# Opening the attention's tile pools beside the last unit of the even layer's projections

## The chip, the cores and the metric

The kernel runs on one core of a Trainium2 chip. It is written with a tile framework: the program says which tiles exist and which instructions read and write them, and a planner puts every engine's instructions into one queue per engine. The core has a matrix engine (TensorE, PE, with a separate row PEld for its weight loads), three engines for elementwise work (VectorE = DVE, ScalarE = ACT, GpSimd = POOL) and SyncE (SP), which here only issues DMA transfers. The matrix engine writes into PSUM, which has eight banks; everything else lies in SBUF, which is shared out in pools of tiles.

The metric is the device time of one execution in microseconds, the median of several. Two profiles are compared by their span.

## The reference

The step runs a hybrid decoder of two layers over a prompt of 2048 tokens and over 8 sampled sequences of 4 tokens each. Layer 0 (the even layer) projects the normalised input once and gives half of the columns to a gated linear recurrence (HGRN2, four heads) and half to forgetting attention (FoX, four heads of 128). Layer 1 (the odd layer) is a second gated recurrence (GLA). What matters here is the attention:

```python
# prompt: causal softmax with a decay bias from the cumulated log forget gates c
logits = q @ k.T * scale + c[t] - c[s]          # masked to s <= t
out = softmax(logits) @ v                       # 16 blocks of 128 queries per head
# sample: the same over 2048 cached positions, gathered by page (16 pages of 128 for each
# of 8 sequences), and over the 4 new ones
out_s = softmax([q @ k_pages.T * scale + suffix, new]) @ [v_pages, v_new]
```

The projection of the even layer has 4 x 512 columns for HGRN2, 4 x 512 for FoX and 4 for the forget gates; afterwards the branches' outputs are joined and multiplied with the layer's output weights.

## The kernel before, in words

**The even layer.** `phase_even` (L1118) works on the prompt in two halves of 1024 tokens (the 32 sample tokens go with the first). For each half the 1024x4100 input weights are taken in 16 *units* of 256 columns, in the order of the list `order` (v0, g0, qf0, ..., Bk0, Bv0, Bk1, Bv1). A unit's product runs as three fp16 matmuls for each 128x128 block (high by high, high by low, low by high, lines L625 to L627 in `mm3`). The 32 units of both halves are numbered 0 to 31. The last, unit 31, is Bv1 of the second half: the value columns of heads 2 and 3. It has four steps of two token tiles; each leaves one PSUM bank of tag `pj` (three banks), which DVE and ACT empty (L1063, L1069, L1070, L1079), and SP stores the fp16 pairs to the scratch tensor `vd` (L1084).

**Key pages beside the units.** The sample's attention reads 128 cached key pages of 256 KB. They are worked on during the units, four pages at a time, 32 times. `KEYS` lists the step numbers (four per unit, 4 * unit + step) at which a load of four pages is issued. `ahead` (L1551) then does the rest at fixed distances: two and three steps later DVE turns the pages (L1526), four steps later the scores are multiplied (L1571), and after each second load the scores are stored five steps later (L1564). Page and turned page lie in the four buffers of tag `wr`, which also hold raw weights during the first half.

**The attention.** `phase_fox` (L1347) opens four pools after the even layer's pools are closed: `fe` and `fx` for tiles in SBUF, `fpa` and `fpb` for PSUM (tags s 2, sc 1; t 2, o 1, kt 2: eight banks). `fox_prompt` (L1365) is a generator for the prompt: for each of four heads, four groups G = 0..3 of 512 queries. A group loads its q, k, bias, v and gate (`loads`, five DMA issues on SP, L1377 to L1392), then for each of four query blocks makes G + 1 score banks (tag `s`), adds the bias and takes the maximum on DVE (L1412), exponentiates on ACT (L1420) and normalises on POOL (L1428). The values of a group (`values`, L1431) are traced among the scores of the next: PE turns the probabilities (L1448), ACT and DVE split them (L1455, L1456), PE multiplies them with v into tag `o`. `fox_sample` (L1598) is the generator for the sample: after a few loads and the masks built on POOL (`past`), it adds the forget bias to the key scores, takes the softmax, and multiplies 2 x 16 sets of four value pages (L1750, called the page steps below) and then the four new positions. Its last step copies and turns the result (L1759, L1762), stores it, and derives a scale for the next projection (L1768 to L1772).

**What sets the order.** Each generator yields a weight after every piece of work. `until(a, ta, b, tb)` draws from a and b so that their sums of weights stay in the proportion ta : tb, and ends when b ends; if a ends first, the rest of b follows. `mux` does the same until both are used up. In `phase_fox` prompt and sample are drawn 270000 : 500000. When the sample is through, `phase_odd` draws what is left of the prompt together with `prepare` (REST_P : REST_S), which loads and splits the first output weight unit (`w_o`: L337, then L355 to L363) and loads and splits the first two pieces of the layer's output `yT` into `act` (L1840, L1847 to L1854). The order of tracing is only a priority: the planner puts an instruction into its engine's queue when its model of time has it ready, the earlier traced first. `issue_after` holds an instruction behind a given one on the same engine. A page step may run ahead of its place, but not before the last matmul that was traced two page steps earlier (VAHEAD = 3).

**Memory.** Pools on the left side of SBUF and on the right side are stacks. Before, the even layer has act, w (three split weight buffers, the four `wr` buffers and small tags) and wl on the right; wk, nrm and stt on the left; and one PSUM pool with pj 3, gr 2, st 1, o 2. A tile in a newly opened pool waits only for the tiles whose bytes it covers.

Of the kernel before, what the change touches and what calls it, by code (L numbers as in the profile page):

```python
# [8 lines left out]
F32 = mybir.dt.float32  # L9
# [6 lines left out]
ALU = mybir.AluOpType  # L16
PSUM = bass.MemoryType.PSUM
DRAM = bass.MemoryType.DRAM

P = 128  # L20
# [18 lines left out]
EWR = 4  # L39
# [9 lines left out]
PG = 6  # L49
KEYS = (*range(4 * 13, 4 * 17, 4), *range(4 * 17, 4 * 31, 2))  # L50
LATER = (*range(4, 14), *range(17, 27))
# [3 lines left out]
FOX_S = 500000.0  # L55
FOX_P = 270000.0
LIN3_A = 40000.0
LIN_E = (20000.0, 15000.0)
# [6 lines left out]
FAR = -3e38  # L65
# [44 lines left out]
def drain(g):  # L110
    for _ in g:
        pass
# [11 lines left out]
class Kern:  # L124
# [993 lines left out]
    def phase_even(self):  # L1118
        tc, nc, i = self.tc, self.nc, self.i
        def pool(name, **kw):  # L1120
            return tc.tile_pool(name=name, bufs=1, reuse_waits="tile", **kw)

        with pool("act", side="right") as ap, pool("w", side="right") as w0, pool("wl", side="right") as wp1, \
                pool("wk") as wp0, pool("nrm") as n0, pool("stt") as sp, pool("ps", space=PSUM) as pp0:
            wpool = self.wpool = Pool(w0, {"w": 3, "wr": EWR, "rm": 3, "pow": 3, "lr": 1})
            wp = Pool(wp0, {"c4": 7, "sam": 1, "v4": 3, "sg": 3, "pd": 1, "kt": 2, "y": EY, "xpad": 1, "vs": 3,
                            "ss": 2, "rs_t": 2, "rs_r": 2, "qz": 1, "scs": 2}, Pool(wp1, {"c2": EC2, "th": ETH}))
            pps = Pool(pp0, {"pj": 3, "gr": 2, "st": 1, "o": 2})
            nrm = Pool(n0, {"th": 1, "nss": 4, "rs_t": 4, "rs_r": 4})
# [7 lines left out]
            last = iter(())  # L1137
# [16 lines left out]
            for hf in range(2):  # L1154
# [89 lines left out]
                last = dense(15, 16)  # L1244
            drain(last)
            for t in range(4 * 32, 4 * 32 + 2):
                self.ahead(wpool, pps, t)

# [78 lines left out]
    def log_sigmoid(self, pool, z, tag):  # L1327
# [17 lines left out]
        nc.vector.scalar_tensor_tensor(zz, q, -2.0, zz, ALU.mult, ALU.add)  # L1345

    def phase_fox(self):  # L1347
        tc, nc = self.tc, self.nc
        self.fox = ExitStack()
        f1, f0 = (self.fox.enter_context(tc.tile_pool(name=x, bufs=2, reuse_waits="tile")) for x in ("fe", "fx"))  # L1350
        pp1, pp0 = (self.fox.enter_context(tc.tile_pool(name=x, bufs=2, space=PSUM, reuse_waits="tile"))
                    for x in ("fpa", "fpb"))
        if True:
            fx = Pool(f0, {"P": 20},
                      Pool(f1, {"caus": 1, "q2": 3, "k2": 6, "cb": 2, "st1": 12, "cm": 2, "th": 4, "tl": 4, "y": 1, "v2": 6, "sg": 3}))
            pps = Pool(pp0, {"t": 2, "o": 1, "kt": 2}, Pool(pp1, {"s": 2, "sc": 1}))
            caus = fx.tile([P, P], F32, tag="caus", name="caus")
            nc.gpsimd.memset(caus, 0.0)
            nc.gpsimd.affine_select(caus, caus, [[-1, P]], ALU.is_ge, FAR, base=0, channel_multiplier=1)
            with tc.tile_pool(name="fs", bufs=1, side="right", reuse_waits="tile") as s0:  # L1360
                fs = Pool(s0, {"pg": PG, "kt": 2})
                self.prompt = self.fox_prompt(fx, pps, caus)
                drain(until(self.prompt, FOX_P, self.fox_sample(fs, pps), FOX_S))

# [233 lines left out]
    def fox_sample(self, fs, pps):  # L1598
# [4 lines left out]
        def one(shape, name, dt=F32):  # L1603
            return fs.tile(shape, dt, tag=name, name=name)
# [41 lines left out]
        def past():  # L1646

            with self.tc.issue_after(self.last_cm.ins):
# [18 lines left out]
                for h in range(NH):  # L1667
# [7 lines left out]
                                        base=0, channel_multiplier=1)  # L1675

            tots = one([P, NH], "tots")
            nc.vector.reduce_sum(tots, lfp.rearrange("p s h -> p h s"), axis=mybir.AxisListType.X)
# [583 lines left out]
```

## Time and profile before

| | |
|---|---|
| median of 3 runs | 2291.44 us (2286.28 to 2295.47) |
| the profiled execution | 2291.65 us |
| its span | 2289.9 us |
| TensorE clock granted, mean | 0.99 |
| PE busy | 2195.9 us (96%) |
| DVE, ACT, POOL busy | 1400.7, 994.3, 724.9 us |
| unit 31's products | 887.8 to 911.4 us |
| attention's first score | 914.5 us |
| first product with the output weights | 1239.0 us |

The span is the time from the first to the last instruction in the trace; the profiled execution lies 0.2 us above the median. A view by windows gives, for each stretch, the time each engine was busy in it with the number of instructions in brackets, then the clock that TensorE was granted (1.00 is full speed), the mean share of the DMA engines that was busy, and GB/s. In a list of instructions the square bracket says how long the engine was idle ahead of the instruction and what released it.

### The profile page before, as it was taken

What the parts mean: (1) busy time and instruction counts of PE and PEld (TensorE: products, weight loads), DVE (VectorE), ACT (ScalarE), POOL (GpSimd) and SP (SyncE); (2) the same over time, 40 slices, a digit from 0 to 9 for tenths busy, and PEclk for the clock granted to TensorE, in tenths of its full rate; (3) what the DMA queues carried; (4) which work ended last, traced back from release to release, by engine and by line L of the source; (5) the groups of instructions that cost most, each with busy time, mean ns of one, the idle gap of its engine ahead of it and who ended that gap; (6) DMA issues with size and microseconds to landing.
All of it is one profiled execution on the core that took longest, in us unless ns stands there. A gap on an engine that the chain in (4) does not pass through costs nothing.

```text
span 2289.9 us, 58071 instructions
## 1 busy us (share of the span) xinstructions
PE 2195.9 (96%) x23316; PEld 1569.0 (69%) x23316; DVE 1400.7 (61%) x3154; ACT 994.3 (43%) x2216; POOL 724.9 (32%) x787
## 2 busy tenths in 40 slices
PE   7999999999999999899999999999999999999998
PEld 5667667774575588455457888677677667567887
DVE  7767677735564466877776454366665655557454
ACT  5434434321221221566667353554644644555243
POOL 2233234100110111544445354154442422232232
PEclk9999999999999999999999999999999999999999
DMA  7444545796575475977735779324325421115554
GB/s 235 144 124 150 160 150 185 233 238 151 159 184 138 118 204 149 280 223 246 223 111 170 260 219 253 101 71 144 92 97 101 120 79 59 54 52 179 171 179 152
DMA packets 361984, 364.02 MB, mean 159 GB/s; under 512 B 108161, under 2 KB 305090, under 8 KB 357490
## 3 DMA queue, kind: packets, MB, share of 16 engines
q1 hardware_dynamic: 359570, 353.69, 52.7%
q0 software_dynamic: 2144, 6.62, 0.8%
q8 instruction: 183, 3.00, 0.6%
q14 instruction: 87, 0.71, 0.1%
HBM read 245.85 MB, written 97.47 MB: 150 GB/s over the span
## 4 chain that ended last, share of the span: by engine, by line
PE 42%; DVE 3%; ACT 2%; DMA 2%; POOL 2%; issue 1%; SPq 0%; POOLq 0%; DVEq 0%; ACTq 0%
PE pt_o L625 4%; PE pt_o L626 4%; PE pt_o L627 4%; PE pt_Cv L625 2%; PE pt_Cv L627 2%; PE pt_Cv L626 2%; PE o_C L909 1%; PE gl_C L756 1%; PE pt L1448 1%; POOL s_C L842 1%; PE py_C L728 1%; ACT L L1420 1%; DMA wr_o<-in_w_out_odd 1%; PE fo L626 0%; PE fo L627 0%
## 5 line engine op out<-in xcount | busy, mean ns | idle before, releaser
L625 PE MATMUL pt_o<-w_o,act 128*128 128x256 f16 x1024 | 279.4, 273 | 1.4 <-ACT sg1C L682 1.4
L626 PE MATMUL pt_o<-w_o,act 128*128 128x256 f16 x1024 | 279.7, 273 | 0.0
L627 PE MATMUL pt_o<-w_o,act 128*128 128x256 f16 x1024 | 279.3, 273 | 0.0
L625 PEld LDWEIGHTS <-act 128*128 128x128 f16 x2304 | 226.1, 98 | 42.3 <-issue 5.3
L626 PEld LDWEIGHTS <-act 128*128 128x128 f16 x2304 | 226.3, 98 | 31.3 <-issue 2.2
L627 PEld LDWEIGHTS <-act 128*128 128x128 f16 x2304 | 226.1, 98 | 31.4 <-issue 2.6
L789 POOL TENSOR_TENSOR kA<-kA,fA 128x512 f32<-128x512 f32 (+1 forms) x56 | 74.2, 1325 | 367.9 <-PE gl_A L756 307.5
L625 PE MATMUL pt_Cv<-w_Cv,act 128*128 128x256 f16 (+1 forms) x512 | 141.5, 276 | 0.9 <-DVE rh L1959 0.8
L627 PE MATMUL pt_Cv<-w_Cv,act 128*128 128x256 f16 (+1 forms) x512 | 141.4, 276 | 0.0
L626 PE MATMUL pt_Cv<-w_Cv,act 128*128 128x256 f16 (+1 forms) x512 | 141.3, 276 | 0.0
L1420 ACT ACTIVATE L<-L,nm,kc 128x512 f32<-128x512 f32 (+3 forms) x160 | 118.2, 741 | 39.4 <-DVE nm L1418 36.1
L1428 POOL TENSOR_SCALAR L<-L,nm 128x512 f32<-128x512 f32 (+3 forms) x160 | 98.2, 629 | 87.4 <-DVE nm L1424 33.7
L789 POOL TENSOR_TENSOR kC<-kC,fC 128x512 f32<-128x512 f32 (+1 forms) x56 | 81.8, 1461 | 136.6 <-PE gl_C L756 93.1
L1455 ACT ACTIVATE th<-pt 128x512 f16<-128x512 f32 (+3 forms) x159 | 80.9, 526 | 74.1 <-PE pt L1448 73.4
L1526 DVE STREAM_TRANSPOSE kt<-kp 128x512 f32<-128x512 f32 x128 | 82.1, 684 | 40.7 <-DMA kp<-in_cache_fox_k 39.7
L1456 DVE TENSOR_TENSOR tl<-pt,th 128x512 f16<-128x512 f32 (+3 forms) x159 | 94.4, 607 | 16.0 <-ACT th L1455 15.0
L1448 PE MATMUL pt<-ident,L 128*128 128x128 f32 x544 | 89.8, 280 | 9.0 <-DVE tl L1456 5.6
L1448 PEld LDWEIGHTS pt<-ident,L 128*128 128x128 f32 x544 | 65.8, 143 | 39.1 <-DVE tl L1456 10.1
L788 DVE TENSOR_TENSOR qC<-qC,fC 128x512 f32<-128x512 f32 (+1 forms) x56 | 72.9, 1302 | 21.1 <-PE gl_C L756 21.1
L1950 ACT ACTIVATE vC<-pt_Cv,kc 128x512 f32<-128x512 f32 (+1 forms) x40 | 23.9, 598 | 134.0 <-PE pt_Cv L627 134.0
L625 PE MATMUL pt_Bv<-w_Bv,act 128*128 128x260 f16 (+1 forms) x256 | 70.8, 277 | 3.9 <-DVE Bvs L1070 3.9
L363 POOL TENSOR_TENSOR w_o<-wr_o,w_o 128x512 f16<-128x512 f32 x32 | 46.5, 1467 | 79.1 <-ACT w_o L362 55.2
(959 smaller groups left out, 6460.4 us busy)
## 6 DMA issues: line engine op xcount, KB each, us to landing
kp<-in_cache_fox_k SPq DMA_DIRECT2D x128, 256.0 KB, 4.9
pgcache_fox_v<-in_cache_fox_v SPq DMA_DIRECT2D x128, 256.0 KB, 4.1
yr<-yT SPq DMA_DIRECT2D x16, 1024.0 KB, 7.0
x1d<-xo SPq DMA_DIRECT2D x44, 256.0 KB, 4.1
wr_o<-in_w_out_even SPq DMA_DIRECT2D x32, 256.0 KB, 5.5
xo<-in_x_prompt SPq DMA_DIRECT2D x32, 256.0 KB, 4.5
wr_Cv<-in_w_in_odd SPq DMA_DIRECT2D x32, 256.0 KB, 3.4
x1r<-x1d SPq DMA_DIRECT2D x16, 512.0 KB, 4.5
```

Source lines behind the costliest of these rows:

```text
L363: nc.gpsimd.tensor_tensor(lo, r, hi, ALU.subtract)
L625: nc.tensor.matmul(ps, lh[0], rh[0], start=first, stop=False)
L626: nc.tensor.matmul(ps, lh[0], rh[1], start=False, stop=False)
L627: return nc.tensor.matmul(ps, lh[1], rh[0], start=False, stop=last)
L788: nc.vector.tensor_tensor(xv[:, :, 1], xv[:, :, 1], t0.to_broadcast([P, nb, w]), ALU.mult)
L789: nc.gpsimd.tensor_tensor(kv[:, :, 0], kv[:, :, 0], t1.to_broadcast([P, nb, w]), ALU.mult)
L1420: self.last_exp = nc.scalar.activation(lt[:, :w], lt[:, :w], AF.Exp, bias=nm[:, 0:1], scale=ib, accum_out=nm[:, 2 + j : 3 + j])
L1428: nc.gpsimd.tensor_scalar(lt[:, :w], lt[:, :w], nm[:, 1:2], 2.0**14, ALU.mult, ALU.mult)
L1448: nc.tensor.transpose(pt[:, w : w + P], rows[b][s // 4][0][:, (s % 4) * P : (s % 4 + 1) * P], self.ident)
L1455: nc.scalar.activation(th[:, a:w], pt[:, a:w], AF.Copy),
L1456: nc.vector.tensor_tensor(tl[:, a:w], pt[:, a:w], th[:, a:w], ALU.subtract)))
L1526: return self.nc.vector.transpose(kt[:, :, 32 * x : 32 * x + 32], t[:, x].rearrange("p (a e) -> p a e", e=32))
```

## The change

The pools of the attention are opened ahead of the last unit instead of after it, and the prompt's generator is drawn beside that unit:

- In `phase_even` the pools are regrouped. The buffers `wr`, `rm`, `pow` and `lr` move from the right side to a new pool on the left; the PSUM tag `pj` (three banks) becomes a pool of its own. The left pools and the other five PSUM banks form an inner group, which is closed once unit 30 and the bias rows (L1312) are traced.
- `fox_open` then opens `fe` and `fx` on the left and one PSUM pool of five banks (t 2, o 1, s 2), and makes the causal mask and the prompt's generator. The tags kt 2 and sc 1, which only the sample and the prompt's end use, get their three banks in `phase_fox`, when `pj` is closed.
- Unit 31 is drawn as `until(self.prompt, FOX_A = 14000, last, 21120)`: the unit's four steps weigh 5280 each, so the prompt is given some 14000 of its weight until the unit has ended. Then `phase_fox` draws prompt and sample 270000 : 500000 as before, both sums starting at zero.
- `KEYS` is moved so that the last key pages are finished with unit 30: the steps were 52, 56, 60, 64, 68, then every second one from 70 to 122; they are 52, 56, 60, then every second one from 62 to 118.
- In `fox_sample`, a yield of 9000 stands between the masks on POOL and the matmuls that use them.

```diff
-KEYS = (*range(4 * 13, 4 * 17, 4), *range(4 * 17, 4 * 31, 2))
+KEYS = (4 * 13, 4 * 14, *range(4 * 15, 4 * 30, 2))
+FOX_A = 14000.0
...
         with pool("act", side="right") as ap, pool("w", side="right") as w0, pool("wl", side="right") as wp1, \
-                pool("wk") as wp0, pool("nrm") as n0, pool("stt") as sp, pool("ps", space=PSUM) as pp0:
-            wpool = self.wpool = Pool(w0, {"w": 3, "wr": EWR, "rm": 3, "pow": 3, "lr": 1})
+                pool("pj", space=PSUM, side="right") as pp1:
+            inner = ExitStack()
+            wk, wp0, n0, sp = (inner.enter_context(pool(x)) for x in ("wr", "wk", "nrm", "stt"))
+            pp0 = inner.enter_context(pool("ps", space=PSUM))
+            wpool = self.wpool = Pool(w0, {"w": 3}, Pool(wk, {"wr": EWR, "rm": 3, "pow": 3, "lr": 1}))
...
-            pps = Pool(pp0, {"pj": 3, "gr": 2, "st": 1, "o": 2})
+            pps = Pool(pp0, {"gr": 2, "st": 1, "o": 2}, Pool(pp1, {"pj": 3}))
...
-            drain(last)
-            for t in range(4 * 32, 4 * 32 + 2):
-                self.ahead(wpool, pps, t)
+            inner.close()
+            self.fox_open()
+            drain(until(self.prompt, FOX_A, last, 21120.0))
...
+    def fox_pool(self, name, **kw):
+        return self.fox.enter_context(self.tc.tile_pool(name=name, bufs=2, reuse_waits="tile", **kw))
+
+    def fox_open(self):
+        nc = self.nc
+        self.fox = ExitStack()
+        f1, f0 = self.fox_pool("fe"), self.fox_pool("fx")
+        fx = Pool(f0, {"P": 20},
+                  Pool(f1, {"caus": 1, "q2": 3, "k2": 6, "cb": 2, "st1": 12, "cm": 2, "th": 4, "tl": 4, "y": 1, "v2": 6, "sg": 3}))
+        self.more_banks = Pool(None, {"kt": 2, "sc": 1})
+        self.fox_banks = Pool(self.fox_pool("fpa", space=PSUM), {"t": 2, "o": 1, "s": 2}, self.more_banks)
+        caus = fx.tile([P, P], F32, tag="caus", name="caus")
+        nc.gpsimd.memset(caus, 0.0)
+        nc.gpsimd.affine_select(caus, caus, [[-1, P]], ALU.is_ge, FAR, base=0, channel_multiplier=1)
+        self.prompt = self.fox_prompt(fx, self.fox_banks, caus)
+
     def phase_fox(self):
...
+        self.more_banks.pool = self.fox_pool("fpb", space=PSUM)
+        with self.tc.tile_pool(name="fs", bufs=1, side="right", reuse_waits="tile") as s0:
+            fs = Pool(s0, {"pg": PG, "kt": 2})
+            drain(until(self.prompt, FOX_P, self.fox_sample(fs, self.fox_banks), FOX_S))
...
+            yield 9000
             tots = one([P, NH], "tots")
```

More of the change, by code (lines that the diff above doesn't have):

```diff
@@ L1345, in log_sigmoid @@
         nc.vector.scalar_tensor_tensor(zz, q, -2.0, zz, ALU.mult, ALU.add)
-    def phase_fox(self):
[L1348 to L1363, printed above, removed]
```

## The prediction

> **What bounds the kernel now.** I read the page first, then windows around the seam between the even layer and the attention, what PE waited for there, and the instructions at the seam.
>
> ```profile
> span 2289.9 us, 58071 instructions
> PE 2195.9 (96%) x23316; PEld 1569.0 (69%) x23316; DVE 1400.7 (61%) x3154; ACT 994.3 (43%) x2216; POOL 724.9 (32%) x787
> ```
>
> PE sets the time: 2195.9 of 2289.9 us. A change that removes no matmul, as this one, can gain only what PE idles or loses to a lowered clock. Where this is, the windows show (columns: PE, PEld, DVE, ACT, POOL busy, granted clock, DMA share, GB/s):
>
> ```profile
> 890.00:911.30 21.30, 21.30 (x240) 18.25 (x237) 11.71 (x22) 3.01 (x7) 2.93 (x5) 1.00 0.48 140
> 911.30:922.00 10.70, 4.73 (x18) 1.66 (x16) 6.26 (x27) 3.37 (x9) 3.51 (x8) 0.68 1.00 265
> 922.00:940.00 18.00, 13.75 (x73) 6.73 (x73) 14.81 (x65) 11.61 (x31) 11.44 (x27) 1.00 1.12 307
> 940.00:950.00 10.00, 7.28 (x44) 4.63 (x44) 6.30 (x23) 6.56 (x18) 9.76 (x22) 1.00 1.02 358
> 950.00:1190.00 240.00, 232.78 (x1600) 128.07 (x1599) 188.25 (x659) 153.63 (x372) 105.89 (x188) 0.99 0.68 210
> 1190.00:1211.00 21.00, 19.72 (x125) 12.12 (x124) 18.14 (x62) 14.11 (x35) 11.56 (x18) 1.00 0.07 23
> 1211.00:1224.00 13.00, 8.26 (x34) 4.40 (x33) 9.92 (x21) 10.10 (x24) 10.41 (x12) 0.67 0.26 78
> 1224.00:1239.00 15.00, 14.87 (x132) 13.53 (x131) 11.69 (x19) 10.07 (x22) 10.45 (x11) 0.94 0.36 108
> ```
>
> Unit 31 runs without a gap (21.30 of 21.30) with DVE a little over half busy. Then three stretches lose time. Counting idle time plus busy time times the missing clock: 911.3 to 922 loses 10.70 - 4.73 + 4.73 x 0.32 = 7.5 us; 922 to 940 loses 4.25; 940 to 950 loses 2.7. Together 14.5 us at the opening. At the other end of the attention 1211 to 1224 loses 4.74 + 8.26 x 0.33 = 7.5 us, and 1224 to 1239 another 1.0.
>
> ```profile
> 911.18 0.27 PE L627 MATMUL pt_Bv<-w_Bv,act 128*128 128x256 f16 x1
> 914.48 0.21 PE L625 MATMUL s<-k,q 128*128 128x128 f16 x1 [3.03 <-DVE Bvs L1070]
> 908.63 1.73 SPq L1384 DMA_DIRECT2D q<-qd  x1
> PE s L625 <- DVE mx L1412: 6.7, 9, 2.6
> PE s L625 <- DVE Bvs L1070: 3.0, 1, 3.0
> PE pt L1448 <- POOL L L1428: 2.6, 3, 1.6
> ```
>
> The last product starts at 911.18 and the first score at 914.48: 3.0 us of waiting, the loads of the first group having been issued from 908.63. The three wait rows (total, times, longest, from 910 to 950) give the rest: 6.7 us in which a score waits for DVE to empty one of two score banks, 2.6 us in which a transposition waits for the normalisation on POOL. The first groups are small: little PE work, a full chain of DVE, ACT and POOL for each query block.
>
> **The change part by part.** Matmuls, DVE and ACT work are the same in number; what moves is their order.
>
> *The two groups among the products.* By the weights that the loops yield, group 0 has 1.6 us of scores and 2.7 of values, group 1 4.2 and 7.0. Drawing 14000 against four steps of 5280 gives 14.7 of weight until the unit ends: group 0 whole, group 1's scores and three of its eight value steps, and the scores of group 2's first two query blocks. So some 15 us of attention work joins 21.3 us of products. DVE is the test: 11.71 us of the unit plus 6.26 + 14.81 from 911.3 to 940 make 32.8 us, against 21.3 + 15 = 36 us of PE. It fits at nine tenths, and the products, with three banks of their own, stand in where a score waits. Therefore the 7.5 us of the first stretch go whole, its clock loss with them. Of the 4.25 us of the second, which is groups 1 and 2, I let 3 go. The 2.7 us from 940 to 950 stay: POOL is full there (9.76 of 10) with the sample's masks, and these are traced behind the unit in both kernels. Against this I set 1.0 us, since chains at nine tenths of DVE will not mesh perfectly. Gain 7.5 + 3.0 - 1.0 = 9.5 us. Bounds: 3 (only the first wait) and 14.5 (all three stretches).
>
> *Loads, masks and pools.* The first three groups' loads, five issues each, move ahead of SP's last `vd` stores and sit at 890 to 911, where the DMA share is 0.48 instead of 1.00 to 1.12; cover enough, counted as nothing. The causal mask is two POOL instructions where POOL is 2.93 of 21.30 busy. `fe` and `fx` now cover the bytes of the `wr` buffers, whose last use is the last key score, in unit 30; the five banks cover those of the bias rows, done at the unit's start. Nothing; if a key score were late, the first group starts a step later and loses part of the 9.5.
>
> *Key pages four steps earlier.* Unit 31 loses its DVE turns, which helps the sum above. The extra loads land in units 15 and 16, at the seam of the two halves:
>
> ```profile
> 460.00:480.00 20.00, 20.00 (x222) 17.27 (x221) 10.94 (x19) 4.68 (x9) 0.00 (x0) 1.00 1.12 218
> 480.00:500.00 20.00, 18.68 (x194) 16.16 (x192) 3.45 (x8) 3.52 (x9) 0.00 (x0) 1.00 1.09 243
> L535 SPq DMA_TRANSPOSE act<-xhl x8: 1810/2494/5348, 460.6 to 490.3; - x8
> L1526 DVE STREAM_TRANSPOSE kt<-kp x128: 660/671/712, 418.5 to 903.3; 128x512 f32<-128x512 f32 x128
> ```
>
> There the DMA engines are already full (1.12, 1.09) and SP carries the eight transposing loads of the next half's activations. Two more sets of four pages, 1 MB each, come into this stretch; at 230 GB/s one is 4.4 us of transfer. PE has 1.3 us of idle there now. If one set delays the last activations by its whole length, 4.4 us are lost; if it falls in a gap, nothing. DVE is free for the eight extra turns (0.67 each). I take 1.0.
>
> *The end of the attention.* This is the part that isn't meant to change and does. Stepping the two loops by their weights: before, the sample's last step is traced with 19 us of the prompt's 233 left, and these 19 are drawn together with `prepare`. After, the prompt starts the joint stretch 14.7 ahead and the sample is 9 longer; the prompt is through before the sample's last step, and `prepare` is traced alone behind both. So the last page step comes later relative to the prompt's end, and with it what follows it:
>
> ```profile
> 1193.94 1.05 PE L1750 MATMUL pv<-vn,pTn 32*16 32x512 f32 x8
> L337 SPq DMA_DIRECT2D wr_o<-in_w_out_even x4: 393/493/526, 1181.6 to 1183.1; - x4
> L359 POOL TENSOR_SCALAR wr_o<-wr_o,kc x2: 1554/1562/1570, 1207.4 to 1209.0; 128x512 f32<-128x512 f32 x2
> L363 POOL TENSOR_TENSOR w_o<-wr_o,w_o x2: 1156/1158/1161, 1213.5 to 1218.2; 128x512 f16<-128x512 f32 x2
> L1847 POOL TENSOR_SCALAR yr<-yr,kc x4: 1558/1807/2097, 1214.7 to 1229.5; 128x512 f32<-128x512 f32 x4
> DMA to landing us min/median/max: 2.6/6.3/11.6
> L1851 POOL TENSOR_TENSOR act<-yr,act x6: 293/1149/1177, 1224.6 to 1238.7; 128x512 f16<-128x512 f32 x4, 128x64 f16<-128x64 f32 x2
> 1226.28 1.18 POOL L1851 TENSOR_TENSOR act<-yr,act 128x512 f16<-128x512 f32 x1
> L625 PE MATMUL pt_o<-w_o,act x1024: 268/273/421, 1239.0 to 2280.8; 128*128 128x256 f16 x171
> PE pt L1448 <- DVE tl L1456: 4.0, 3, 1.6
> ```
>
> Before, the last page step is at 1193.94, the preparation starts on POOL at 1207.4 and has the first piece ready at 1227.5, and the first product is at 1239.0: 11.5 us of slack. The price is paid inside: the preparation shares ACT, DVE and POOL with the prompt's last softmax, and 4.0 us of waits for L1456 are the core of the 7.5 us lost from 1211 to 1224. After, the last page step may run once the matmuls of two page steps earlier are through, which by the weights leaves 16.4 us of prompt values behind it, about 18 with its own 1.05. The last softmax is then over before the preparation; I let the 7.5 us go. But the preparation takes 20 us as it ran (1207.4 to 1227.5), and at least 3.1 + 2.3 + 3.6 + 2.3 = 11.4 us of POOL alone. If it starts 13.5 us behind the page step as now, it ends 25 to 33.5 us behind it, and PE has 18 us of work: a gap of 7 to 15.5 us. If it starts as soon as its weights have landed (issued 12.3 us ahead of that page step, at 1181.6), there is no gap. A gap also lowers the clock:
>
> ```profile
> 1214.00:1216.00 2.00, 0.38 (x3) 0.06 (x1) 2.00 (x3) 0.74 (x2) 2.00 (x2) 0.87 0.00 0
> 1216.00:1218.00 2.00, 1.81 (x5) 0.67 (x5) 2.00 (x6) 0.38 (x1) 2.00 (x2) 0.50 0.04 8
> ```
>
> The clock falls to 0.50 behind idle pieces of which the longest is 1.6 us (the wait row above), and costs 8.26 x 0.33 = 2.7 us. I take a middle between the two starts, a gap of 5.5 us with 2.7 of clock: 8.2 lost against 7.5 gained, rounded to 0.5 lost. Bounds: 7.5 gained; 15.5 + 2.7 - 7.5 = 10.7 lost.
>
> The Trainium skill ("TensorE: Matmul & The Clock Gate", Part 1: The HAM clock gate) has the clock halved only after an idle window of about 3.4 us. The half clock is what the rows show; the window isn't, for no single wait at 1211 to 1218 is that long. By that rule a gap shorter than the window would be free of the 2.7 us; were the middle gap one, the sum below would be -10.7 instead of -8.0.
>
> **Sum.** -9.5 + 1.0 + 0.5 = -8.0 us against the profiled execution's 2291.65, which lies 0.2 above the median: **2283.5 us**.
>
> **The rivals.** *Both ends gain.* The preparation starts when its weights land and is hidden beneath the last values. For it: its load needs no result of the sample, and POOL, at 0.55 busy from 1190 to 1211, has room. Against it: the weights landed some 20 us before POOL took them up now. -9.5 + 1.0 - 7.5 = -16: 2275.7 us.
>
> *The end costs more than the start gives* (the other side). The preparation stays tied to the sample's end. Gap 15.5, clock 2.7; then the second piece, which needs the raw buffer back (a load of 6.3 us, the landing row's median, and 3.6 + 2.3 us of POOL against 21.3 / 4 = 5.3 us of product): about 7 more. 15.5 + 2.7 + 7 - 7.5 = 17.7 lost, -9.5 + 1.0 + 17.7 = +9.2: 2300.9 us. It decides from a gap of about 13 us on (9.5 - 1.0 + 7.5 - 2.7). For it: POOL's queue holds the sample's four stores ahead of L359 now. Against it: the planner tends to fill idle engines.
>
> *The change doesn't do what it says.* PE takes its matmuls in the order of its queue: at 914.48 two scores' work and everything behind waits. A score put among the products by a model that has its loads or DVE earlier than they are makes the products wait too, and the 6.7 us of bank waits only move into the unit. Then only the 3.0 us go: -3.0 + 1.0 + 0.5 = 2290.2 us. For it: DVE at nine tenths; against it: three banks of products as reserve.
>
> The Trainium skill speaks for this rival: by "TensorE: Matmul & The Clock Gate", in the table at its head, only weight loads are pulled ahead of matmuls in flight. The wait rows agree, each with PE standing until the score's bank was free.
>
> **How the numbers follow.** My forecast 0.46, both ends 0.26, the end loses 0.15, nothing moved 0.13. Less than 0.5% (11.5 us, 2280.2 to 2303.1) can hardly be told from no change here. The forecast's own range is 2278 to 2289, of which a fifth lies under 2280.2: 0.09. Both ends adds nearly all of its 0.26: 0.35 faster. Slower takes over half of the third case and a little for queues that come out otherwise downstream: 0.12. Same 0.53. The range reaches from 2272 (start at its bound of 14.5 with the end near clean) to 2300 (most of the end's loss).
>
> **What would show it.** Right: from the start of unit 31 to group 2's scores no idle piece of 3 us and no clock under 0.9; no wait for L1456 among the last softmax; the key loads at 470 to 500 with PE idle under 3 us. The end is read from the last fo product to the first pt_o product: under 2 us, both ends gain; over 13, the end loses. Wrong: scores that wait among the unit's products in the sum of 5 us, or a preparation on POOL that begins only after the sample's stores.

## The result, and the profile after

The changed kernel takes 2298.64 us (median of 20 runs, 2291.60 to 2305.55), the kernel before 2290.16 us beside it (20 runs, 2284.10 to 2298.96). The ratio is 1.0037 with a 95% interval of 1.0025 to 1.0048: slower by some 8.5 us, where 8 us of gain were forecast. The time lies inside the range given; the direction is the opposite one.

The profiled execution has these totals; PE has the same work as before:

```profile
span 2299.0 us, 58081 instructions
PE 2195.9 (96%) x23316; PEld 1571.7 (68%) x23316; DVE 1400.7 (61%) x3154; ACT 995.6 (43%) x2216; POOL 725.5 (32%) x787
```

So the 9.1 us of span are idle time or lowered clock. The windows of the changed kernel (columns as before: PE, PEld, DVE, ACT, POOL busy, granted clock, DMA share, GB/s) show where:

```profile
480.00:520.00 40.00, 27.59 (x275) 20.02 (x274) 10.44 (x19) 5.72 (x14) 0.00 (x0) 0.91 0.92 214
...
911.00:922.00 11.00, 9.96 (x89) 8.30 (x87) 5.17 (x21) 2.67 (x8) 4.16 (x8) 1.00 1.04 263
922.00:940.00 18.00, 15.82 (x119) 11.19 (x117) 15.32 (x58) 10.37 (x27) 9.44 (x17) 0.99 1.17 255
940.00:950.00 10.00, 9.25 (x44) 4.68 (x44) 8.29 (x34) 7.06 (x19) 5.49 (x10) 0.84 1.11 353
950.00:1000.00 50.00, 43.26 (x365) 27.44 (x364) 40.62 (x160) 30.87 (x76) 28.84 (x58) 0.98 0.52 170
1190.00:1224.00 34.00, 32.18 (x208) 16.80 (x207) 25.92 (x74) 23.12 (x56) 12.33 (x21) 0.99 0.21 71
1224.00:1243.00 19.00, 18.41 (x155) 16.26 (x154) 14.97 (x37) 11.33 (x20) 12.05 (x15) 0.94 0.08 25
1243.00:1262.00 19.00, 13.98 (x104) 10.86 (x104) 7.75 (x10) 11.84 (x22) 15.22 (x13) 0.82 1.06 339
```

Two stretches that the prediction did not show, in the kernel before:

```profile
480.00:520.00 40.00, 38.28 (x316) 25.74 (x314) 7.74 (x16) 8.31 (x17) 0.00 (x0) 1.00 0.94 216
950.00:1000.00 50.00, 49.49 (x436) 30.14 (x435) 42.98 (x166) 31.25 (x75) 21.65 (x38) 1.00 0.62 203
```

The loss of a stretch is again idle time plus busy time times the missing clock. The seam of the two halves, 480 to 520, loses 12.4 + 27.59 x 0.09 = 14.9 us, against 1.7 before: **13.2 us more, and the largest difference in the kernel**. The opening, 911 to 950, loses 5.6 against 14.5: 8.9 less. The 50 us behind it lose 7.6 against 0.5: 7.1 more. The end, 1190 to 1262, loses 11.4 against 10.7 (from 1190 to 1245): 0.6 more before rounding.

What stands at the seam is one instruction. PE's list there, in the changed kernel (start, duration, engine, line; the bracket is the idle time ahead and its releaser):

```profile
507.87 0.38 PE L628 MATMUL pf_Ag<-act,w_Ag 128*128 128x512 f16 x1
517.05 1.94 PE L1579 MATMUL ks<-kt,qz 128*32 128x128 f32 x32 [8.80 <-DVE kt L1534]
518.92 0.61 PE L626 MATMUL pf_Ag<-act,w_Ag 128*128 128x512 f16 x1
```

A key score `ks` stands between two products of the same unit, `pf_Ag`, and holds the second for 8.80 us. The product behind it needs nothing from the score: the same tiles had been multiplied at 507.87. DVE's turns and SP's issues of pages and activations in the same kernel say what the score waited for:

```profile
514.50 2.49 DVE L1534 STREAM_TRANSPOSE kt<-kp 128x512 f32<-128x512 f32 x4 [17.45 <-DMA scd<-scs]
518.33 1.30 DVE L1534 STREAM_TRANSPOSE kt<-kp 128x512 f32<-128x512 f32 x2 [0.76 <-DMA kp<-in_cache_fox_k]
```

```profile
483.75 1.89 SPq L1530 DMA_DIRECT2D kp<-in_cache_fox_k  x4
485.75 4.96 SPq L536 DMA_TRANSPOSE act<-xhl  x1
...
491.94 5.33 SPq L536 DMA_TRANSPOSE act<-xhl  x2
...
501.57 8.98 SPq L1530 DMA_DIRECT2D kp<-in_cache_fox_k  x8
```

DVE had nothing to do for 17.45 us and then turned the pages in 2.5. The pages were late: after the four at 483.75, SP issued transposing loads of activations and some stores, and the next eight pages, two sets, came only from 501.57 on and took SP 8.98 us. (The row at 514.50 names the store of the scores that was issued next in SP's queue; the turns read only pages, so I take the last page as the true releaser.) In the kernel before the sets stood further apart there, and the waits for turned pages were short. PE's wait rows from 478 to 530 (total, times, longest), after and before:

```profile
PE ks L1579 <- DVE kt L1534: 9.4, 2, 8.8
PE pt_Av L626 <- DMA act<-xhl: 2.1, 3, 1.3
```

```profile
PE ks L1571 <- DVE kt L1526: 1.0, 2, 0.6
```

### The profile page after: what moved, and what is told of

The parts are those of the page before. It is cut to its first block, busy times and chain, and to the rows that moved or that the text cites. A ratio compares the mean times of both kernels' runs of the same rounds, so it can differ in the third digit from the quotient of the medians.

```text
span 2299.0 us, 58081 instructions
## 1 busy us (share of the span) xinstructions
PE 2195.9 (96%) x23316; PEld 1571.7 (68%) x23316; DVE 1400.7 (61%) x3154; ACT 995.6 (43%) x2216; POOL 725.5 (32%) x787
## 4 chain that ended last, share of the span: by engine, by line
PE 47%; DVE 3%; DMA 3%; ACT 2%; POOL 2%; issue 2%; SPq 1%; POOLq 0%; DVEq 0%; ACTq 0%
PE pt_o L626 4%; PE pt_o L628 4%; PE pt_o L627 4%; PE pt L1456 2%; PE pt_Cv L626 2%; PE pt_Cv L628 2%; PE pt_Cv L627 2%; PE pv L1759 1%; PE gl_C L757 1%; PE o_C L910 1%; PE fo L626 1%; PE fo L627 1%; PE fo L628 1%; PE s L626 1%; PE s L628 1%
## 5 line engine op out<-in xcount | busy, mean ns | idle before, releaser
L1464 DVE TENSOR_TENSOR tl<-pt,th 128x512 f16<-128x512 f32 (+3 forms) x159 | 95.3, 608 | 14.7 <-ACT th L1463 12.9
L626 PE MATMUL pt_Av<-w_Ai,act 128*128 128x256 f16 x256 | 70.5, 275 | 3.5 <-DMA act<-xhl 2.1
```

Of the source, the lines that this page charges most:

```text
L626: nc.tensor.matmul(ps, lh[0], rh[0], start=first, stop=False)
L1464: nc.vector.tensor_tensor(tl[:, a:w], pt[:, a:w], th[:, a:w], ALU.subtract)))
```

## The experiments

Theory: the new load steps of the key pages make the kernel slower, because key scores stand in PE's queue ahead of their pages; the opening's gain is real but partly given back. Rivals: the transfers themselves are what is short at the seam; the end is what costs; the opening's gain is kept or lost as a whole. Losses below are worked out as above, from windows like those shown. The table's are from the windows 440 to 520, 911 to 950 with 950 to 1000, and 1190 to 1224 with 1224 to 1265; the clock has two digits, so other windows give sums that differ by up to 0.8 us (the opening before is 15.0 above and 15.8 here). A ratio is always to the kernel before, with its 95% interval. Two runs can hardly be told apart when their ratios differ by less than some 0.15% (an estimate from the intervals).

| run | ratio | 440–520 | 911–1000 | 1190–1265 |
|---|---|---|---|---|
| before | 1 | 1.7 | 15.8 | 10.6 |
| the change | 1.0037 [1.0025, 1.0048] | 15.1 | 13.0 | 11.6 |
| b_keys | 1.0033 [1.0018, 1.0048] | 9.6 | 10.3 | 10.8 |
| a_early | 1.0017 [1.0000, 1.0033] | 5.2 | 13.2 | 12.1 |
| a_ratio | 1.0015 [1.0001, 1.0029] | 14.0 | 10.9 | 9.1 |
| a_noyield | 1.0052 [1.0036, 1.0069] | 15.3 | 12.7 | 12.3 |
| a_late | 0.9987 [0.9971, 1.0002] | 5.3 | 12.9 | 11.8 |
| a_both | 1.0013 [0.9999, 1.0027] | 5.2 | 14.6 | 8.0 |
| a_both_y | 1.0020 [1.0006, 1.0035] | 7.4 | 10.6 | 6.6 |
| a_both_none | 1.0012 [0.9998, 1.0026] | 7.5 | 14.9 | 7.4 |
| a_late_ratio | 0.9978 [0.9968, 0.9988] | 3.9 | 11.2 | 8.8 |
| b_keys_late | 1.0025 [1.0013, 1.0037] | 4.5 | 20.3 | 11.0 |
| a_early_late | 0.9973 [0.9961, 0.9984] | 0.0 | 10.2 | 12.5 |
| a_nomask | 0.9973 [0.9962, 0.9985] | 5.2 | 12.1 | 7.9 |
| a_early_late_none | 0.9987 [0.9974, 1.0000] | 0.9 | 16.6 | 7.3 |
| b_early_late | 1.0016 [1.0005, 1.0027] | 0.0 | 13.9 | 10.6 |

The losses come from one execution each, the ratios from 10 to 20. One execution can lie well off its median (the profiled span of b_early_late is 2280.0 us, its median 2293.37), so a loss tells where time moved, best where a named wait stands behind it, and the ratio decides what it is worth.

**b_keys: the load steps alone**, in the kernel before.

```diff
-KEYS = (*range(4 * 13, 4 * 17, 4), *range(4 * 17, 4 * 31, 2))
+KEYS = (4 * 13, 4 * 14, *range(4 * 15, 4 * 30, 2))
```

> The kernel before with only the new KEYS. Theory 1 (the key pages at the seam): of the 9 us by which the change is slower, the two page sets that moved into units 15 and 16 cost the most: a key score stands in PE's queue ahead of unit 17's products while its pages are still on the way. Then 480 to 520 us loses some 13 to 15 us here too (1.7 in the kernel before), and the time is before plus 11 to 13 us, a ratio of 1.005. Rival (the regrouped pools): the wr buffers' new place or the pools' new waits are behind it; then this kernel is within 2 us of before.

1.0033, less than the 1.005 expected, and still nearly all of the slowdown from one line of the change. The windows and PE's waits at the seam of this run:

```profile
480.00:520.00 40.00, 32.58 (x315) 24.07 (x314) 12.65 (x23) 6.42 (x15) 0.00 (x0) 0.93 0.98 230
```

```profile
PE ks L1571 <- DVE kt L1526: 5.0, 2, 4.4
```

The stretch loses 7.4 + 32.58 x 0.07 = 9.7 us, with the same wait in it, shorter by half.

**a_early: the extra sets elsewhere.** The changed kernel with the two extra sets at the steps 54 and 58, in the units 13 and 14, so that the seam keeps the spacing of before.

```diff
-KEYS = (4 * 13, 4 * 14, *range(4 * 15, 4 * 30, 2))
+KEYS = (*range(4 * 13, 4 * 15, 2), 4 * 15, 4 * 16, *range(4 * 17, 4 * 30, 2))
```

> The changed kernel with two of the 32 page sets moved from steps 62 and 66 to steps 54 and 58, so that the seam of the halves carries the same sets as before (60, 64, 68) and the last is still 118. Theory 1: 480 to 520 us loses 2 to 4 us instead of 14.9; the time is 10 to 12 us under the changed kernel, a ratio to before of 0.998 to 1.000, unless units 13 and 14 now wait in turn. Rival (the regrouped pools): ratio stays at 1.0037.

1.0017: half of the slowdown goes, short of the 0.998 to 1.000 expected, though 440 to 520 loses 5.2 us instead of 15.1. The two runs say where the time goes, and not yet why: this edit leaves less to transfer at the seam and brings the pages earlier, both at once.

**a_late: only the place of the score.** The changed kernel with its own load steps; the scores of the sets loaded at the steps 60 to 70 are traced five steps behind the load instead of four (and their stores six instead of five). Pages, turns and transfers stay.

```diff
+SLOW = range(60, 71)
...
-        if t - 4 in KEYS:
-            j, g = divmod(KEYS.index(t - 4), 2)
+        d = t - 4 if t - 4 not in SLOW else -1
+        d = t - 5 if t - 5 in SLOW else d
+        if d in KEYS:
+            j, g = divmod(KEYS.index(d), 2)
```

> The changed kernel, with the scores of the key sets loaded at the steps 60 to 70 placed one step (5.3 us of products) later than in the changed kernel; pages, turns and everything else stay. Theory (a key score standing in PE's queue ahead of products whose inputs are there, 8.8 us at 517.05): the wait falls by one step to some 3.5 us, the stretch 480 to 520 loses 7 to 10 us instead of 14.9, and the ratio to the kernel before falls from 1.0037 to about 1.001 to 1.002. Rival (the transfers are what is short there, and PE runs out of activations whichever score stands in front): 480 to 520 still loses 13 us or more, with PE waiting for the activations' loads, ratio 1.003 to 1.004.

0.9987: 0.50% under the change, some 11 us, from one step of place in a queue. The issues, the turns and the score in this run, then PE's waits from 478 to 530, then the window:

```profile
503.31 6.30 SPq L1531 DMA_DIRECT2D kp<-in_cache_fox_k  x8
512.07 2.49 DVE L1535 STREAM_TRANSPOSE kt<-kp 128x512 f32<-128x512 f32 x4 [16.34 <-DMA kp<-in_cache_fox_k]
515.80 1.08 PE L1584 MATMUL ks<-kt,qz 128*32 128x128 f32 x32
```

```profile
PE pt_Av L627 <- DMA act<-xhl: 3.7, 2, 2.5
PE pt_Av L627 <- DVE Bvs L1072: 1.6, 1, 1.6
```

```profile
480.00:520.00 40.00, 34.70 (x318) 23.44 (x317) 12.25 (x22) 7.04 (x16) 0.00 (x0) 1.00 0.97 218
```

The eight pages are issued 1.7 us later than in the changed kernel (503.31), and the score runs only 1.25 us earlier (515.80 against 517.05). But there is no bracket in front of it and no row for `ks` among the waits: products stood ahead of it. With the turns done at 512.07 + 2.49 = 514.56, a score right behind 507.87 would still have held PE for some 6 us (an estimate from these rows). The stretch loses 5.3 us, of which 3.7 are the wait for activations that the rival named; so that rival has a part, the smaller one. The theory holds, and the gain is larger than expected (1.001 to 1.002).

**a_ratio: only the end.** The changed kernel with a weight that again leaves 19 us of prompt when the sample is through.

```diff
-FOX_P = 270000.0
+FOX_P = 246000.0
```

> The changed kernel with prompt and sample drawn 246000 : 500000 instead of 270000 : 500000, by which the sample's last step again has 19 us of the prompt's weight left behind it, as before the change. Theory 2 (the end): the gap of 5 us behind the first products with the output weights, and its clock, come from the preparation being traced behind everything; then the gap goes, the last softmax again shares the engines with the preparation, and the time is 0 to 5 us under the changed kernel. Rival: the page steps closer together earlier on cost what the end gains, no change within 2 us.

1.0015, 0.22% under the change, with intervals that just overlap. In the changed kernel the end reads so (the first two lines are PE's, the other two from the chain that ended last):

```profile
1244.99 0.28 PE L626 MATMUL pt_o<-w_o,act 128*128 128x256 f16 x1 [1.48 <-ACT act L1859]
1248.74 0.39 PE L626 MATMUL pt_o<-w_o,act 128*128 128x256 f16 x1 [3.35 <-ACT act L1862]
```

```profile
1241.13 1.17 POOL w_o L364
1242.32 5.62 DMA yr<-yT
```

The preparation's weights and its second piece are on the chain, and PE waits 3.35 us for that piece. With the ratio changed, the products run on:

```profile
1245.00:1265.00 20.00, 20.00 (x198) 16.90 (x196) 6.45 (x12) 14.16 (x25) 6.08 (x8) 1.00 1.06 365
```

**a_noyield: without the yield of 9000.**

```diff
-            yield 9000
```

> The changed kernel without the new yield of 9000 behind the masks. Theory 3 (the gather): the 2.6 us that a transposition of the gathered log forget values waits for its load on PE, and what follows from 950 to 1000 us (7.6 us lost, 0.5 before), come from the planner placing it ahead of the load's real landing; the yield made this less, so without it that wait is 3 to 6 us and the time 0 to 4 us longer. Rival: the yield shifts the whole sample by 5 us of prompt and so costs at the end; without it the gap behind the first output products is shorter and the time 2 to 4 us less.

1.0052, 0.15% over the change, with intervals that overlap. The wait for the gather is 2.7 us, where 3 to 6 were expected, and 2.6 with the yield. No harm of the yield is seen; whether it helps is not shown.

**a_both: a_early and a_ratio together** (both diffs above).

> The changed kernel with two edits together: the two extra key sets loaded at the steps 54 and 58 instead of 60-62 and 64-66 (so that the seam keeps the spacing that it had before), and FOX_P 246000, which by the weights leaves 19 us of the prompt for the preparation, as before the change. Alone they measured 1.0017 and 1.0015 against 1.0037 for the change. Theory (three separate places of loss): the two add up, -0.20% and -0.22% from 1.0037, ratio 0.999 to 1.000, 2289 to 2291 us. Rival (the saved time is taken by the next wait downstream, so only one of them counts): 1.0015.

1.0013: they do not add up (0.999 to 1.000 was expected), though the seam keeps its 5.2 us and the end loses 8.0 instead of 11.6. Part of the difference stands where the extra sets now begin: 340 to 440 loses 15.5 us here, 11.1 in the changed kernel, and one wait there is new:

```profile
PE pt_Bk L626 <- DVE Bvs L1071: 2.3, 1, 2.3
```

All seven runs with the early load steps have it between 340 and 440 (2.0 to 3.3 us), and none of the nine others. What takes up the rest is not shown; 911 to 1000 loses 14.6 here.

**a_both_none: the pools open early, the groups don't.** Against a_both:

```diff
-FOX_P = 246000.0
-FOX_A = 14000.0
+FOX_P = 264500.0
+FOX_A = 1.0
```

> As the run with both edits, with FOX_A 1 (next to nothing of the prompt is traced among unit 31's products; the pools still open ahead of it) and FOX_P 264500, which again leaves about 19 us of prompt at the sample's end. Theory (the opening gains 9 us and gives 7 of them back by 1000): 911 to 950 loses some 14 us as before the change, 950 to 1000 about 1, and the ratio is 0.05 to 0.1% above the run with both edits. Rival (the 9 us are kept, and the loss from 950 on has other grounds): 950 to 1000 still loses 6 us or more and the ratio is 0.35 to 0.4% above that run.

1.0012, the same time. The windows, a_both first:

```profile
911.00:950.00 39.00, 34.98 (x230) 23.02 (x229) 31.29 (x119) 23.05 (x60) 21.12 (x42) 0.96 1.11 301
950.00:1000.00 50.00, 43.92 (x361) 27.73 (x363) 40.15 (x159) 28.02 (x68) 27.56 (x52) 0.93 0.43 136
```

```profile
911.00:950.00 39.00, 28.79 (x180) 18.32 (x178) 24.06 (x91) 15.65 (x41) 18.29 (x40) 0.88 0.93 247
950.00:1000.00 50.00, 49.24 (x416) 29.80 (x415) 43.41 (x175) 32.11 (x79) 25.05 (x46) 0.99 0.67 211
```

With the groups the first stretch loses 5.4 us instead of 13.7, and the second 9.2 instead of 1.3. In this pair the opening's gain is given back within 50 us.

**a_both_y: the sample's masks and gather given more time.** Against a_both:

```diff
-FOX_P = 246000.0
+FOX_P = 237000.0
...
-            yield 9000
+            yield 25000
```

> As the run with both edits, with the yield behind the masks 25000 instead of 9000 and FOX_P 237000, so that the sample's first matmuls come some 8 us later among the prompt's groups and the sample still ends with 19 us of prompt left. Theory (what the opening gained is given back at 950 to 1000 because the sample's gather and masks have had less time): the waits of lfT for lfp (2.6) and of psf for mpg (1.2) go, 950 to 1000 loses under 4 us instead of 7.6, ratio some 0.15% under the run with both edits. Rival (the give-back is the softmax work on DVE and POOL that the groups of the opening leave behind): 950 to 1000 still loses 6 us or more, and the ratio is within 0.1% of that run.

1.0020, not better. In the changed kernel these stand in the stretch that gives back:

```profile
938.37 0.39 PE L626 MATMUL s<-k,q 128*128 128x512 f16 x1 [1.76 <-DVE mx L1420]
...
957.57 0.39 PE L1691 MATMUL lfT<-ident,lfp 128*128 128x128 f32 x1 [2.55 <-DMA lfp<-in_cache_fox_logf,pcol]
960.63 0.49 PE L1695 MATMUL psf<-tots,mpg 128*128 128x128 f32 x2 [1.15 <-POOL mpg L1668]
```

In a_both_y the wait for the gather is 0.7 us and that for the mask is gone, and 950 to 1000 still loses 5.8 us. But in a_both, from which this run differs, they already were 0.8 us and none, and the stretch lost 9.2. So the give-back does not need these two waits, and the theory of the late gather falls.

**a_late_ratio: a_late and FOX_P 246000.**

> The changed kernel with the scores of the sets loaded at the steps 60 to 70 one step later (0.9987 alone) and FOX_P 246000 (1.0015 against 1.0037 for the change, alone). Theory (the seam and the end are separate places): both count, ratio 0.996 to 0.998, 480 to 520 loses about 5 us and 1245 to 1265 nothing. Rival (the end's saving is taken up by the opening's and the prompt's softmax, as it nearly was where FOX_P went together with other load steps, 1.0013): 0.9985 or more.

0.9978, within what was expected (0.996 to 0.998). It lies 0.09% under a_late, inside the intervals, so whether the end's part counts too is not shown.

**a_nomask: as a_late_ratio, without the 14 affine selections on POOL** that shape the sample's masks, so that its results for the sample are not the reference's. For example:

```diff
-                nc.gpsimd.affine_select(stri, stri, [[-1, P]], ALU.is_gt, 0.0, base=0, channel_multiplier=1)
```

> As the run with the later scores and FOX_P 246000, with the 14 affine selections left out that build the sample's masks on POOL (6.2 us of POOL at 940 to 1000; the memsets stay, and the sample's part of the result is computed with wrong masks). Theory (from 950 on POOL's masks stand between the prompt's normalisations, where before they stood in the idle opening): 950 to 1000 loses 3 us or less and the ratio is 0.15 to 0.2% under that run. Rival (the loss is the chain from maximum to normalised probabilities of the larger groups, which comes in any order): 950 to 1000 still loses 5 us or more, ratio within 0.1%.

0.9973, within 0.1% of a_late_ratio; 950 to 1000 loses 3.6 us against 4.1. The masks on POOL are not what gives the gain back. The larger groups' chain from maximum to normalised probabilities is what is left of the causes named here, by exclusion and not by a run of its own.

**b_keys_late: the load steps with the later scores, in the kernel before.**

> The kernel before with the changed kernel's load steps alone (1.0033), and on top of it the scores of the sets loaded at the steps 60 to 70 one step later. Theory (the held products are the whole price of the load steps): the 4.4 us wait of a score for its turned page goes, 480 to 520 loses about 5 us instead of 9.7, ratio 1.000 to 1.0015. Rival (the later score helps only beside the rest of the change): 1.003 again.

1.0025. In the stretch it is as the theory says (4.5 us instead of 9.6, no wait of a score), in the time it isn't (1.000 to 1.0015 expected). Part of it is seen: among PE's waits from 880 to 1000 stands

```profile
PE lfT L1687 <- DMA lfp<-in_cache_fox_logf,pcol: 5.1, 1, 5.1
```

where b_keys waits 1.7 us, and the whole opening loses 20.3 us instead of 10.3. The gather is not issued later there: POOL issues it at 927.7 and DVE first reads it at 936.7, 9.0 us on, against 941.4 and 947.3 in b_keys, 5.9 us. Why it takes longer is open. So in the kernel before, the held products are not shown to be the price of the load steps.

**a_early_late: all three**: a_early's steps, a_late's rule for the steps 52 to 70, FOX_P 246000.

> As the run with the later scores and FOX_P 246000, and the load steps 52, 54, 56, 58, 60, 64, 68 and then every second one (the seam's own spacing as before the change), with the scores of all sets from 52 to 70 one step later. Theory (scores that stand in PE's queue ahead of their pages are what the seam costs, and the seam's transfers the rest): 440 to 520 loses 3 us or less, ratio 0.2% under that run. Rival (the pages at 52 to 58 take their transfers' time from the units 13 and 14 instead): 340 to 440 loses some 4 us more than the change, no gain over that run.

0.9973 [0.9961, 0.9984], 2285.32 us: **faster than both kernels**. The seam is whole:

```profile
440.00:520.00 80.00, 80.00 (x835) 63.63 (x834) 36.95 (x73) 15.97 (x35) 0.00 (x0) 1.00 0.97 233
```

The 0.2% under a_late_ratio that the theory wanted are not there (0.05%, inside the intervals); the units 13 and 14 take some back (340 to 440 loses 14.5 us here, 12.7 in a_late_ratio).

**a_early_late_none and b_early_late** take a_early_late apart: the first has FOX_A 1 and FOX_P 264500, the second is the kernel before with the load steps and later scores of a_early_late alone.

> As the run with early load steps, later scores and FOX_P 246000 (0.9973), with FOX_A 1 and FOX_P 264500: the pools open ahead of unit 31, next to nothing of the prompt is traced among its products, and the preparation again finds 19 us of prompt. Theory (the opening's 9 to 10 us are mostly given back by 1000, net 1 to 5 us): 911 to 1000 loses 13 to 15 us instead of 10.2, ratio 0.998 to 0.9995. Rival (with the seam mended they are kept): ratio 1.001 or more.

> The kernel before, with the load steps 52, 54, 56, 58, 60, 64, 68 and then every second one to 118 and the scores of the sets from 52 to 70 one step later; nothing else of the change. Theory (mended load steps are worth nothing by themselves, since the kernel before loses only 1.7 us at the seam; what the mended change gains is the opening and the end): 440 to 520 loses under 2 us, 911 to 1000 some 15 us as before, ratio 0.999 to 1.001. Rival (the load steps are the gain): 0.998 or less.

The first is at 0.9987, as the theory had it: the groups among the products are worth 0.14%, some 3 us, with intervals that overlap. In its windows 911 to 1000 loses 16.6 us against 10.2 (most of the gain is kept up to 1000 in this pair), and 1190 to 1265 gets 5.2 of these back (7.3 against 12.5). The second is at 1.0016, slightly outside the 0.999 to 1.001 expected and far from the rival's 0.998: mended load steps gain nothing by themselves. From there to a_early_late lie 0.43%, about 10 us, which the rest of the change and the new FOX_P bring together. The larger part of it, 0.29%, is there already in a_early_late_none, without the groups among the products; whether the early pools, the yield or FOX_P bring it, no run tells.

## Why the prediction was wrong, point by point

**The key pages: the step that failed.** It took 1.0 us, with 4.4 us as the most (4.6 with four pages of 256 KB counted in full), "if one set delays the last activations by its whole length". The load steps alone cost 0.33% (7.6 us), and in the changed kernel the seam lost 13.2 us more. The step costed the transfers and asked who needs the activations. It did not ask what stands behind a late page: a turn on DVE, behind it a score at a fixed distance in PE's queue, and behind that the rest of a unit's products. The size of that wait isn't bounded by one set's transfer; it is the whole delay of the pages less the distance left for them. The loads of activations on SP ahead of the pages were in the quoted rows (eight of them, 460.6 to 490.3), and that they would hold the pages, rather than the pages them, could have been read from that.

How far the held products are shown to be the cause: in the changed kernel, moving the scores alone gives back 0.50%, all of the slowdown. In the kernel before, the same edit gives 0.08%, which can't be told from nothing, so there the 7.6 us are measured but not explained. Of the 16.5 us between the forecast (8.0 less) and the medians (8.5 more), this term makes 6.6 by b_keys (7.6 instead of 1.0); most of the rest is the opening's.

**The rival that had the mechanism had it in the wrong place.** "The change doesn't do what it says" named a score that is put among products by a model that has its loads earlier than they are, and makes the products wait too. That is what happened, to a key score in unit 17 and not to an attention score in unit 31. The page that the rival named, the Trainium skill, "TensorE: Matmul & The Clock Gate", the table at its head, names weight loads as what is pulled ahead of matmuls in flight. The trace agrees: 8.80 us with products behind the score, which in a_late run ahead of it. Of the three wait rows that the rival took as its witness, one (2.6 us) is a transposition waiting for POOL and not a score waiting for its bank.

**The opening: the stretch right, the sum wrong.** 9.5 us were predicted, and 911 to 950 lost 8.9 us less; no idle piece of 3 us was left, as the test asked, though the clock was at 0.50 once, from 940 to 942. But the term ended at 950 and the give-back begins there: 7.1 us by 1000. With and without the groups, and FOX_P set to leave the end alike, two pairs of runs give 0.01% the wrong way and 0.14% the right way: 0 to 3 us in place of 9.5. Neither is clear of nothing, and neither reaches 9.5 us (0.41%) even at the far ends of its intervals. The table agrees: 911 to 1000 loses 12.1 us in the mean of the ten executions with the groups (10.2 to 14.6) and 15.3 in the mean of the six without (10.3 to 20.3). The prediction's own test of DVE ("fits at nine tenths") looked at the work up to 940 only. The first two groups are the cheap ones; drawing them forward makes the next ones, with the sample's start among them, follow sooner. That this is the reason is a reading, and no run isolates it.

**The end: the size right, the way to it not.** 0.5 us of loss were predicted and 0.6 measured, waits and a lower clock against the gain of a calm last softmax. The term was a middle between two starts of the preparation on POOL, 13.5 us behind the last page step or as soon as the weights land. The late one came, with the sign of being wrong that the prediction gave for it, a preparation that begins only after the sample's stores (`ys`):

```profile
1219.73 1.05 PE L1759 MATMUL pv<-vn,pTn 32*16 32x512 f32 x8
1229.28 1.07 POOL L1777 DMA_DIRECT2D yT<-ys  x2
1234.97 3.13 POOL L360 TENSOR_SCALAR wr_o<-wr_o,kc 128x512 f32<-128x512 f32 x2
```

It starts 15.2 us behind the page step. PE, however, is kept for 22.7 us behind that step (1219.73 to 1242.41), where 18 were counted, and then finds a first part of the preparation done. So the two errors nearly cancel, and the match is luck. The loss itself is no chance: four executions of the table with the old end lose 10.6 to 11.0 us from 1190 to 1265, and four with the changed one 11.6 to 12.3. The test for the term was badly chosen, too. It read the end from the gap between the last value product and the first product with the output weights, and there is none:

```profile
1242.41 0.22 PE L628 MATMUL fo<-th,v 128*128 128x128 f16 x1
1242.46 0.27 PE L626 MATMUL pt_o<-w_o,act 128*128 128x256 f16 x1
```

By "under 2 us" both ends would have gained. The weights come just in time (1241.13 + 1.17 = 1242.3), and the waits stand behind that first product, the longest (3.35 us) for the second piece, which the prediction had only in its third case. So the sum of this term was right and its place wasn't. What a better ratio gains here is not settled: 0.22% from the change to a_ratio, 0.04% from a_early to a_both, 0.09% from a_late to a_late_ratio, each within what the intervals leave open; 2.5, 4.1 and 3.0 us by the losses.

**Loads, masks and pools at nothing**: nothing in the runs speaks against it; there is 1.0 us of waiting for `k` in the opening. **The sum.** -8.9 + 7.1 + 13.2 + 0.6 = +12.0 us by these stretches, 9.1 by the spans, 8.5 by the medians. The difference lies in stretches whose rows were too coarse to divide. One of them is known, and costs: between 520 and 880 the changed kernel loses 4 us more than before, half of it in one wait of `gl_A` for DVE's `qA` (2.5 us from 800 to 840, 0.5 before). The load steps alone have it too (2.3 us), but a_noyield, with the same load steps, has only 0.4, so whose it is stays open. With these 4 us the stretches make 16, and some 7 must come back where the rows do not show them. Open stays also what the opening's give-back consists of, and what besides the new wait of 2.0 to 3.3 us keeps a_early's gain from adding to a_ratio's.

## What to carry to other kernels

Where work is put among another loop's matmuls at a fixed distance behind its loads, price a late load by what stands behind the matmul that waits, not by the transfer: ask for each such instruction what is next in its engine's queue. One step more of distance cost nothing that was seen in the changed kernel, and moving a load is not the same as moving its consumer. And carry a gain past the stretch in which it appears: the same work done earlier brings the next, heavier work forward, and only the end of the stage says what is left.

## What the runs showed of the hardware

The granted clock does not follow the length of a single wait. In the changed kernel (windows of 2 us):

```profile
938.00:940.00 2.00, 1.21 (x8) 0.76 (x9) 1.96 (x8) 1.76 (x4) 1.67 (x3) 0.93 1.11 359
940.00:942.00 2.00, 1.71 (x5) 0.60 (x5) 1.23 (x8) 1.17 (x4) 1.02 (x2) 0.50 1.12 367
942.00:944.00 2.00, 1.81 (x9) 0.95 (x8) 1.29 (x5) 1.71 (x7) 0.77 (x2) 0.72 1.09 366
...
956.00:958.00 2.00, 0.43 (x3) 0.41 (x4) 0.46 (x1) 0.01 (x1) 0.31 (x2) 1.00 0.99 299
958.00:960.00 2.00, 1.48 (x11) 0.93 (x9) 2.00 (x6) 1.43 (x4) 1.88 (x3) 1.00 1.00 363
```

A wait of 1.76 us with one of 0.71 close behind it halves the clock at 940; the longer one of 2.55 us, up to 957.57, leaves it at 1.00. By the shares of the first three rows the half clock lasts about 3.4 us (0.28 + 2.00 + 1.12, an estimate that takes the clock as either 1.00 or 0.50). At the seam the clock is at 0.50 before the 8.80 us of waiting end, and at 1.00 again 3 us after work resumes (517.05):

```profile
514.00:516.00 2.00, 0.00 (x0) 0.00 (x0) 1.50 (x3) 0.00 (x0) 0.00 (x0) 0.50 0.86 333
...
520.00:522.00 2.00, 2.00 (x11) 0.91 (x10) 0.00 (x0) 0.00 (x0) 0.00 (x0) 1.00 1.05 219
```

The Trainium skill ("TensorE: Matmul & The Clock Gate", Part 1: The HAM clock gate) halves the clock after an idle window of about 3.4 us. The seam agrees with that; the drop at 940, with no wait over 1.76 us, does not if the window has to be one wait, and there the measurement decides. A price of clock for a gap of 1.8 to 2.6 us can thus be told only as a chance.
